# Summing the last expert's part on the residual in PSUM, in a two-layer trunk on one core

## The chip, the cores and the metric

The kernel runs on one core of one Trainium2 chip, as one launch. Its time is the device time of that core in microseconds (us); of a kernel several runs are taken, and the median stands for it. All engines of the core work from their own instruction queues, in order: TensorE (PE, with its weight loads shown as PEld), VectorE (DVE), ScalarE (ACT), GpSimd (POOL) and SyncE (SP), which issues most of the transfers.

## The reference, cut to what matters

Two layers. Layer 1 ends with a top-2-of-8 expert mixer, a layer norm over a scaled residual, and a gated embedding:

```python
def moe_swiglu(h, w_router, w1, w3, w2):
    ...
    for e in range(N_EXPERTS):
        out = out + gates[:, e:e + 1] * swiglu(t, w1[e], w3[e], w2[e])

# in reference(), layer i
f = moe_swiglu(x, router_w[j], exp_w1[j], exp_w3[j], exp_w2[j])
x = layer_norm(DEEPNORM_ALPHA * x + f, ln2_g[i], ln2_b[i])
x = x + jax.nn.sigmoid(x @ ple_gate_w[i]) * (p[i] @ ple_w[i])
```

There are 256 tokens, 1024 channels, 3584 hidden channels in an expert. Everything is float32 at its ends.

## The kernel before

The tokens are worked in two halves of 128 (`h` = 0, 1), each a tile of 128 partitions by 1024 channels, and the channels in two parts of 512 (`c` = 0, 1), since one PSUM bank holds 512 float32 a partition. A product of two float32 values is made from parts: weights and activations are split into a high part of the type fp32r and a rest (`H`, `L`), and a product is two or three passes over these (L343, L345 or L343, L347, L348). Weights that are not split (`direct`) go as plain float32 (L340). Weights come in 1 MB transfers into slots of one pool (`w`), ScalarE copies the high part (L143), VectorE makes the rest (L158); `W.prepare` says at which place of the program this is queued.

The experts run in blocks of 512 hidden channels. Tokens are gathered for an expert by a product with a 0/1 selection, and its result is scattered back by a product with the transposed selection `selTs`. `evacuate` splits the sum of an expert's down products into `y.h` (tile `cat`) and `y.l` (tile `yc`). `scatter` makes, for each half and part, two products into a PSUM bank `ps_sc` (L808, L809) and has VectorE add it to the residual `yacc` in SBUF (L811). `yacc` starts as the scaled residual, so after the last scatter it holds what the last norm works on.

The end of layer 1, in `moe`, stands in this order, which is the order of each engine's queue (nothing reorders it):

1. scatter of the last expert for half 0, `norm_begin` on `yacc[0]`: statistics (L383), mean and variance (L385, L387), the power on GpSimd (L389)
2. three of the four embedding products `ps_ple` (`emit(3)`), and 20 products that only keep TensorE busy (`warm`, L308)
3. `norm_apply` part by part (L412 with the mean and the gain, L413 with the inverse deviation and the offset), after each part the transposes (`tr`, L331) and their split into `xH`, `xL` (L316, L317) with an unsplit copy (L319)
4. scatter of the last expert for half 1, the fourth embedding product (copied out by ScalarE at L440), the statistics of half 1, `norm_apply` of half 1 (both parts)
5. `embed_gate`: four gate products `ps_gate`, the first with split weights (half 0, part 0), then half 0 part 1 with direct weights; the transposes of half 1 lie inside it; then half 1. `combine` ends each: sigmoid (L1150), multiply, add (L1151, L1152), and the transfer to the output.

PSUM has eight banks here: four for `mmt` tiles, used in turn, and four named `acc0` to `acc3`. A call of `acc` without a number takes the next of the four; a call with a number takes that one. A bank that is taken anew waits until its former content has been read. Up to the last `embed_gate` there are 38 calls without a number (14 in each mixer, 4 in the dense layer, 4 in the first `embed_gate`, 2 in `moe`), so its first product takes `acc2`, and the next ones `acc3`, `acc0`, `acc1`, `acc2`.

Of the kernel before, what the change touches and what calls it, by code (L numbers as in the profile page):

```python
# [13 lines left out]
ALU = mybir.AluOpType  # L14
# [179 lines left out]
def trunk(ctx: ExitStack, tc: tile.TileContext, a: dict, out: bass.AP):  # L194
    nc = tc.nc
# [9 lines left out]
    def acc(name, k=None):  # L205

        if k is None:
            k = at[0] % 4
            at[0] += 1
        return pacc.tile([P, 512], F32, tag=f"acc{k}", name=name)  # L210

    def mmt(name):
        return pmm.tile([P, 512], F32, tag="mm", name=name)

    def tl(tag, shape, dt=F32):
        return ap.tile([P] + shape, dt, tag=tag, name=tag)
# [73 lines left out]
    ident = con[:, C_ID:C_ID + P]  # L290
# [19 lines left out]
    def table(func):  # L310

        nc.scalar.activation(dummy, neghalf, func)

    def split_into(dst, src):

        nc.scalar.copy(dst.h, src)  # L316
        nc.vector.tensor_sub(dst.l, src, dst.h.bitcast(F32))  # L317
        if dst.f is not None:
            nc.scalar.copy(dst.f, src)  # L319

    def new_xT(f=None):
        return [Split(tl(f"xH{h}", [KD, P], F32R), tl(f"xL{h}", [KD, P], F32R), None if f is None else f[:, h])
                for h in range(2)]
# [10 lines left out]
    def to_xT(dst, src, c):  # L334

        split_into(dst[:, 4 * c:4 * c + 4, :], transposes(src[:, c * 512:(c + 1) * 512], 4))
# [43 lines left out]
    def norm_scalars(srcs):  # L380
        st = sm.tile([P, 2, 6], F32, tag="st", name="st")
        for i, s_ in enumerate(srcs):
            nc.vector.bn_stats(st[:, i], s_())  # L383
        mv = sm.tile([P, 2], F32, tag="mv", name="mv")
        nc.vector.bn_aggr(mv, st[:, :len(srcs)].rearrange("p a b -> p (a b)"))  # L385
        ve = sm.tile([P, 1], F32, tag="ve", name="ve")
        nc.vector.tensor_scalar_add(ve, mv[:, 1:2], EPS)  # L387
        rs = sm.tile([P, 1], F32, tag="rs", name="rs")
        nc.gpsimd.tensor_tensor(rs, ve, neghalf, op=ALU.pow)  # L389
        return mv[:, 0:1], rs  # L390
# [7 lines left out]
    def norm_begin(x, psums, between=None):  # L398

        cs = [x[:, c * 512:(c + 1) * 512] for c in range(2)]  # L400
        def add(c):
            if c and between:
                between()
            if psums is not None:
                nc.vector.scalar_tensor_tensor(cs[c], cs[c], ALPHA, psums[c], op0=ALU.mult, op1=ALU.add)
            return cs[c]
        return norm_scalars([lambda: add(0), lambda: add(1)])

    def norm_apply(gb, x, scalars, c):
        cs = slice(c * 512, (c + 1) * 512)  # L410
        mu, rs = scalars
        nc.vector.scalar_tensor_tensor(x[:, cs], x[:, cs], mu, gb[0][:, cs], op0=ALU.subtract, op1=ALU.mult)  # L412
        nc.vector.scalar_tensor_tensor(x[:, cs], x[:, cs], rs, gb[1][:, cs], op0=ALU.mult, op1=ALU.add)  # L413

    def norm(gb, x, psums):
        sc = norm_begin(x, psums)
        for c in range(2):
            norm_apply(gb, x, sc, c)
# [379 lines left out]
    def evacuate(accs):  # L798
        y = Split(tl("cat", [2, 512], F32R), tl("yc", [2, 512], F32R))
        for c in range(2):  # L800
            split_into(y[:, c, :], accs[c])
        return y

    def scatter(selT, y, yacc, k, halves=(0, 1)):
        for h in halves:
            for c in range(2):
                ps = acc("ps_sc", k + h) if c else mmt("ps_sc")
                nc.tensor.matmul(ps, selT[:, h], y.h[:, c], start=True, stop=False)  # L808
                nc.tensor.matmul(ps, selT[:, h], y.l[:, c], start=False, stop=True)  # L809
                yo = yacc[h][:, c * 512:(c + 1) * 512]  # L810
                nc.vector.tensor_add(yo, yo, ps)  # L811
# [27 lines left out]
    def moe(l, xr, gb1, mix, project):  # L839
        xT = new_xT()  # L840
        wrs = tl("s0", [KD, 2, NE], F32R)
        split_into(Split(wrs[:, :, 0], wrs[:, :, 1]), wr)
        project(0)
        norm(gb1, xr[0], mix[0])
        project(1, lambda k: k == 1 and to_xT(xT[0], xr[0], 0))
        sc = norm_begin(xr[1], mix[1], lambda: to_xT(xT[0], xr[0], 1))
        for c in range(2):
            norm_apply(gb1, xr[1], sc, c)
        table(AF.Sigmoid)

        p1 = [acc("p1") for _ in range(2)]
        lg = tl("lg", [2, NE])

        pr = [mmt("ps_r") for _ in range(2)]

        def router(h, ks):

            for k in ks:
                nc.tensor.matmul(pr[h][:, :2 * NE], xT[h].h[:, k, :], wrs[:, k].rearrange("p a e -> p (a e)"),
                                 start=k == 0, stop=False)  # L860
                nc.tensor.matmul(pr[h][:, :NE], xT[h].l[:, k, :], wrs[:, k, 0], start=False, stop=k == KD - 1)

        ids = W.names["w1e0_0"]
        proj(ids, p1[0], xT[0])
        to_xT(xT[1], xr[1], 0)
        router(0, range(KD))
        to_xT(xT[1], xr[1], 1)
        W.prepare("w3e0_0", 2)
        routed = []

        def routing(k):
            if k < 2:
                router(1, range(4 * k, 4 * k + 4))
            if k == 1:
                for h in range(2):
                    nc.vector.tensor_copy(lg[:, h], pr[h][:, NE:2 * NE])
                    nc.vector.tensor_add(lg[:, h], lg[:, h], pr[h][:, :NE])
                routed.extend(route(lg))
            if k == KP:
                gate, msk = routed  # L880
                routed.extend(positions(msk, gate, xr))

        proj(ids, p1[1], xT[1], free=True, also=routing)
        gate, msk, posm, cnt = routed
        sel, cc = select(0, posm, gate, 0, 0)
        W.prepare("w3e0_0")
        W.hl = HL_SECOND
        ss = [silu(p1[h], 512, h) for h in range(2)]
        W.cap = W.names[f"gate1{l}"][-1] + 1
        selT, gsl = turn_select(sel, 0), gate_select(sel, cc, 0)  # L890
        xg = gather(sel, xr, 0)
        ps = mmt("ps_s")
        for h in range(2):
            nc.tensor.matmul(ps, sel[:, h], ss[h], start=h == 0, stop=h == 1)
        s_ = tl("g1", [512])
        nc.scalar.copy(s_, ps)
        (ranks, gates), beyond, ci = order(cnt, posm, gate)
        p3 = mmt("p3")
        both("w3e0_0", [p3], [xg])
        g = glu(s_, p3, 512, 0, gsl)  # L900
        W.hl = HL_MOE
        yacc2 = W.temp([2, D])
        yacc = [yacc2[:, h] for h in range(2)]
        late = {}

        def end(c):

            if c == PLE_AT:
                late["ple"] = embedding(l)
            if c == GAINS_AT:  # L910
                late["gains"] = gains(l, "ln2", D)
            if c == FE:
                W.prepare(f"ple{l}", None)
                late["ple"][2]()

        last = experts(ranks, gates, xr, yacc, (selT, gsl, xg), lambda: hidden(g, 512, 0),
                       lambda: over(ci, beyond, gate, xr, yacc), end)
        gb, (ple, emit, _) = late["gains"], late["ple"]
        xT2 = new_xT(W.temp([2, KD, P]))
        table(AF.Sigmoid)  # L920
        last(0)
        sc = [norm_begin(yacc[0], None)]
        W.prepare(f"gate0{l}", 1)
        emit(EM[0])
        keep_warm(20)
        norm_apply(gb, yacc[0], sc[0], 0)
        to_xT(xT2[0], yacc[0], 0)
        norm_apply(gb, yacc[0], sc[0], 1)
        W.prepare(f"gate0{l}", 2)
        to_xT(xT2[0], yacc[0], 1)  # L930
        emit(EM[1])
        last(1)
        W.prepare(f"gate0{l}", 3)
        emit(4 - EM[0] - EM[1])
        sc.append(norm_begin(yacc[1], None))
        W.prepare(f"gate0{l}", 4)
        for c in range(2):
            norm_apply(gb, yacc[1], sc[1], c)
        W.prepare(f"gate1{l}")
        return xT2, yacc, lambda c: to_xT(xT2[1], yacc[1], c), ple  # L940

# [97 lines left out]
    def experts(ranks, gates, xr, yacc, nxt, first, more, end):  # L1039
# [4 lines left out]
        selTs, state = [nxt[0], None], {0: nxt[1:]}  # L1044
# [4 lines left out]
        for i, (e, c) in enumerate(BLOCKS):  # L1049
# [39 lines left out]
            pe, pc, paccs, pgT = prev  # L1089
# [46 lines left out]
        pe, pc, paccs, pgT = prev  # L1136
        down(W.names[f"w2e{pe}_{pc}"], paccs, pgT, False, True, True)
        end(FE)
        y = evacuate(paccs)
        return lambda h: scatter(selTs[1], y, yacc, 2 * (pe % 2), (h,))  # L1140

    def embed_gate(l, xT, late, xr, ple, last):

# [175 lines left out]
```

## Time and profile before

| | |
|---|---|
| median of 3 runs | 1354.1 us (1352.34 to 1355.91) |
| the profiled execution | 1351.87 us |
| its span, from the first to the last instruction | 1350.0 us |
| TensorE busy | 1314.0 us, 97% of the span |
| VectorE busy | 1169.0 us, 87% |
| ScalarE busy | 920.9 us, 68% |
| mean granted TensorE clock | 0.996 |

Busy time of an engine is the union of its instructions' times. The share of the whole span says what kind of kernel it is; what the end of the program costs is read from the timeline of its last 50 us, engine by engine, and from what ended the idle time ahead of an instruction. The granted clock is 1.00 where TensorE runs at its full level of 2.4 GHz and 0.5 at its lower one of 1.2 GHz.

### The profile page before, as it was taken

Reading aid. Unit: us, or ns where it says so; the run is one execution under the profiler, and the core shown is the slowest. Engines: PE = TensorE matmul, PEld = TensorE weight load, DVE = VectorE, ACT = ScalarE, POOL = GpSimd, SP = SyncE. Lnnn points to the kernel's source line nnn. Section 1 sums busy time; section 2 is a strip of 40 time slices with the busy share of each in tenths; the row PEclk is TensorE's granted clock in tenths of the full one; section 3 lists DMA queues with packets and bytes.
Section 4 is the critical chain, followed back from the end, with each engine's and each line's share of the span. In section 5 each row is a group of like instructions: output and inputs, shape, how many; then the busy total and the mean of one; then the engine's idle time right before and its main releaser. Section 6 shows DMA issues by size and latency. Waiting matters only on the chain. (4 is left out here: it accounts for less than half of the span.)

```text
span 1350.0 us, 17064 instructions
## 1 busy us (share of the span) xinstructions
PE 1314.0 (97%) x6310; PEld 1078.3 (80%) x6310; DVE 1169.0 (87%) x1098; ACT 920.9 (68%) x864; POOL 18.4 (1%) x31
## 2 busy tenths in 40 slices
PE   9999999999999999999999999999999999999788
PEld 7878888888868888878888878888887888888656
DVE  6987544567888989999999999999999999999874
ACT  6435444436425778878888887888887888898652
POOL 0000000010000000000000000000000000000000
PEclk9999999999999999999999999999999999999899
DMA  9546555446654889999999999999999999999850
GB/s 367 221 137 242 213 187 187 164 138 252 222 187 154 322 333 421 421 401 377 420 414 383 421 420 372 411 420 405 393 420 402 379 420 406 399 373 419 358 217 31
DMA packets 62171, 433.09 MB, mean 321 GB/s; under 512 B 6960, under 2 KB 7472, under 8 KB 11008
## 3 DMA queue, kind: packets, MB, share of 16 engines
q1 hardware_dynamic: 60336, 425.60, 79.9%
q0 software_dynamic: 1168, 4.23, 1.0%
q10 hardware_dynamic: 576, 2.10, 0.4%
q8 instruction: 51, 0.84, 0.2%
q14 instruction: 40, 0.33, 0.1%
HBM read 430.85 MB, written 1.05 MB: 320 GB/s over the span
## 5 line engine op out<-in xcount | busy, mean ns | idle before, releaser
L158 DVE TENSOR_TENSOR w<-w 128x2048 fp32r<-128x2048 f32 (+1 forms) x456 | 886.5, 1992 | 57.7 <-ACT w L143 51.0
L143 ACT CAST w<-w 128x2048 fp32r<-128x2048 f32 (+1 forms) x456 | 746.8, 1677 | 125.6 <-PE p L347 41.5
L343 PE MATMUL p<-w,xH 128*128 128x512 f32 (+1 forms) x1096 | 432.5, 395 | 7.5 <-DVEq L1034 6.0
L347 PE MATMUL p<-w,xH 128*128 128x512 f32 (+1 forms) x648 | 249.1, 384 | 0.4 <-DVE w L158 0.4
L348 PE MATMUL p<-w,xL 128*128 128x512 f32 (+1 forms) x648 | 249.5, 385 | 0.0
L343 PEld LDWEIGHTS p<-w,xH 128*128 128x128 f32 x1096 | 206.8, 189 | 49.4 <-issue 6.6
L343 PE MATMUL y<-w,gH 128*128 128x512 f32 x448 | 175.4, 392 | 2.5 <-DVE gH L378 2.5
L345 PE MATMUL p<-w,xH 128*128 128x512 f32 x448 | 175.9, 393 | 0.0
L348 PEld LDWEIGHTS p<-w,xL 128*128 128x128 f32 x648 | 121.8, 188 | 24.7
L347 PEld LDWEIGHTS p<-w,xH 128*128 128x128 f32 x648 | 122.0, 188 | 24.2 <-DVE w L158 0.8
L343 PEld LDWEIGHTS y<-w,gH 128*128 128x128 f32 x448 | 84.1, 188 | 20.9 <-DVE gH L378 3.6
L345 PEld LDWEIGHTS p<-w,xH 128*128 128x128 f32 x448 | 85.1, 190 | 17.0
L348 PE MATMUL y<-w,gL 128*128 128x512 f32 x224 | 87.4, 390 | 0.5 <-DVE gL L317 0.5
L347 PE MATMUL y<-w,gH 128*128 128x512 f32 x224 | 87.3, 390 | 0.0
L345 PE MATMUL y<-w,gH 128*128 128x512 f32 x224 | 87.3, 390 | 0.0
L483 DVE SCALAR_TENSOR_TENSOR yc<-w,vec,yc 128x256 f32<-128x256 f32 x176 | 70.4, 479 | 0.0
L646 ACT ACTIVATE s<-p 128x512 f32<-128x512 f32 (+1 forms) x69 | 41.1, 599 | 24.3 <-PE p L348 24.3
L316 ACT CAST gH<-tr 128x512 fp32r<-128x512 f32 x38 | 21.9, 588 | 47.9 <-PE tr L331 47.3
L317 DVE TENSOR_TENSOR gL<-tr,gH 128x512 fp32r<-128x512 f32 x38 | 25.7, 685 | 32.7 <-ACT gH L316 32.7
L348 PEld LDWEIGHTS y<-w,gL 128*128 128x128 f32 x224 | 42.1, 188 | 9.6 <-DVE gL L317 0.9
L347 PEld LDWEIGHTS y<-w,gH 128*128 128x128 f32 x224 | 42.1, 188 | 9.0
L345 PEld LDWEIGHTS y<-w,gH 128*128 128x128 f32 x224 | 42.1, 188 | 8.6
(227 smaller groups left out, 1391.7 us busy)
## 6 DMA issues: line engine op xcount, KB each, us to landing
w<-in_exp_w SPq DMA_DIRECT2D x336, 1024.0 KB, 8.8
w<-in_dense_w SPq DMA_DIRECT2D x33, 1024.0 KB, 5.1
w<-in_w_out SPq DMA_DIRECT2D x8, 1024.0 KB, 8.7
w<-in_ple_gate_w SPq DMA_DIRECT2D x8, 1024.0 KB, 5.9
w<-in_w_gv SPq DMA_DIRECT2D x6, 1024.0 KB, 6.9
w<-in_w_u SPq DMA_DIRECT2D x4, 1024.0 KB, 10.5
w<-in_w_gv SPq DMA_DIRECT2D x4, 512.0 KB, 6.8
w<-in_w_small SPq DMA_DIRECT2D x2, 1024.0 KB, 10.1
```

Source lines behind the costliest of these rows:

```text
L143: nc.scalar.copy(h, w)
L158: engine.tensor_tensor(l, w, h.bitcast(F32), op=ALU.subtract)
L316: nc.scalar.copy(dst.h, src)
L317: nc.vector.tensor_sub(dst.l, src, dst.h.bitcast(F32))
L343: nc.tensor.matmul(ps, x.h, wh, start=start, stop=False)
L345: nc.tensor.matmul(ps, x.h, wl, start=False, stop=stop)
L347: nc.tensor.matmul(ps, x.h, wl, start=False, stop=False)
L348: nc.tensor.matmul(ps, x.l, wh, start=False, stop=stop)
L483: nc.vector.scalar_tensor_tensor(yc[:, ct], src, weight(ct, t), yc[:, ct], op0=ALU.mult, op1=ALU.add)
L646: nc.scalar.activation(s_[:, :nf], p1[:, :nf], AF.Silu)
```

## The change

Only the last expert's scatter and the norm behind it are touched. Instead of a product into `ps_sc` and an addition on VectorE, a bank `ps_sum` first takes the residual itself, as a product of `yacc` with the identity in plain float32 (`residual`), and then the two selection products on top. The norm's statistics and the first step of `norm_apply` read that bank. The four VectorE additions are gone. For half 0 the identity products are queued ahead of `evacuate`; for half 1 they stand directly ahead of its selection products. The banks are named by number: `acc0` and `acc1` for half 0, `acc2` and `acc3` for half 1. Lines from 409 on move: L412 and L413 become L413 and L414, L440 becomes L441, L1150 becomes L1169.

```diff
-    def norm_apply(gb, x, scalars, c):
+    def norm_apply(gb, x, scalars, c, src=None):
         cs = slice(c * 512, (c + 1) * 512)
+        src = x[:, cs] if src is None else src
         mu, rs = scalars
-        nc.vector.scalar_tensor_tensor(x[:, cs], x[:, cs], mu, gb[0][:, cs], op0=ALU.subtract, op1=ALU.mult)
+        nc.vector.scalar_tensor_tensor(x[:, cs], src, mu, gb[0][:, cs], op0=ALU.subtract, op1=ALU.mult)
...
-        last(0)
-        sc = [norm_begin(yacc[0], None)]
+        sums = [last(0)]
+        sc = [norm_scalars([lambda c=c: sums[0][c] for c in range(2)])]
...
-        norm_apply(gb, yacc[0], sc[0], 0)
+        norm_apply(gb, yacc[0], sc[0], 0, sums[0][0])
...
-        last(1)
+        sums.append(last(1))
...
-        sc.append(norm_begin(yacc[1], None))
+        sc.append(norm_scalars([lambda c=c: sums[1][c] for c in range(2)]))
...
+        sums = {}
+        def residual(h):
+            sums[h] = [acc("ps_sum", 2 * h + c) for c in range(2)]
+            for c in range(2):
+                nc.tensor.matmul(sums[h][c], ident, yacc[h][:, c * 512:(c + 1) * 512], start=True, stop=False)
+        def last(h):
+            if h:
+                residual(h)
+            for c in range(2):
+                nc.tensor.matmul(sums[h][c], selTs[1][:, h], y.h[:, c], start=False, stop=False)
+                nc.tensor.matmul(sums[h][c], selTs[1][:, h], y.l[:, c], start=False, stop=True)
+            return sums[h]
+        residual(0)
         y = evacuate(paccs)
-        return lambda h: scatter(selTs[1], y, yacc, 2 * (pe % 2), (h,))
+        return last
```

TensorE's queue behind the transposes of half 0, part 1, in the difference of the two programs (- before, + now; `ps_sc` and `ps_sum` are the PSUM banks, `w` is the residual `yacc`, `con` holds the identity, `cat` and `yc` the split result of the expert; in brackets the engines waited for, _49 being part of a semaphore's name):

```order
 L331 MATMUL tr<-con,w 128x128 x3
-L808 MATMUL ps_sc<-cat,m_9306 128x512 [waits PE_49]
-L809 MATMUL ps_sc<-yc,m_9306 128x512
-L808 MATMUL ps_sc<-cat,m_9306 128x512
-L809 MATMUL ps_sc<-yc,m_9306 128x512
+L1146 MATMUL ps_sum<-w,con 128x512 x2
+L1153 MATMUL ps_sum<-cat,m_9306 128x512
+L1154 MATMUL ps_sum<-yc,m_9306 128x512
+L1153 MATMUL ps_sum<-cat,m_9306 128x512
+L1154 MATMUL ps_sum<-yc,m_9306 128x512
 L343 MATMUL ps_ple<-w 128x512 [waits PE_49]
```

Two identity products are new between the transposes and the selection products; for half 0 the same two stand between the last down product and the selection products.

TensorE's queue at the first gate product of half 0 (`ps_gate_13550`; the weights `w_13423` and `w_13502` are its first and second quarter), before:

```order
L343 MATMUL ps_gate_13550<-w_13423,xH0_13401 128x512 [waits Activation_49]
L347 MATMUL ps_gate_13550<-w_13423,xH0_13401 128x512
L348 MATMUL ps_gate_13550<-w_13423,xL0_13402 128x512
L343 MATMUL ps_gate_13550<-w_13423,xH0_13401 128x512
L347 MATMUL ps_gate_13550<-w_13423,xH0_13401 128x512
L348 MATMUL ps_gate_13550<-w_13423,xL0_13402 128x512
L343 MATMUL ps_gate_13550<-w_13502,xH0_13401 128x512 [waits Activation_49]
L347 MATMUL ps_gate_13550<-w_13502,xH0_13401 128x512 [waits DVE_49]
```

and now:

```order
L343 MATMUL ps_gate_13550<-w_13423,xH0_13405 128x512 [waits DVE_49,Activation_49]
L347 MATMUL ps_gate_13550<-w_13423,xH0_13405 128x512
L348 MATMUL ps_gate_13550<-w_13423,xL0_13406 128x512
L343 MATMUL ps_gate_13550<-w_13423,xH0_13405 128x512
L347 MATMUL ps_gate_13550<-w_13423,xH0_13405 128x512
L348 MATMUL ps_gate_13550<-w_13423,xL0_13406 128x512
L343 MATMUL ps_gate_13550<-w_13502,xH0_13405 128x512 [waits Activation_49]
L347 MATMUL ps_gate_13550<-w_13502,xH0_13405 128x512
```

The first product has a wait for VectorE that it did not have, and the waits for VectorE at the rests of the three later quarters of the weights are gone.

VectorE's queue for half 1, before (`ps_sc_13513` and `ps_sc_13517` are the scattered parts, `w_3562` the residual, `mv` and `rs` the norm's scalars, `w_13523` and `w_13543` the third and fourth quarter of the gate's weights):

```order
L811 TENSOR_TENSOR w_3562<-w_3562,ps_sc_13513 128x512 [waits PE_49]
L811 TENSOR_TENSOR w_3562<-w_3562,ps_sc_13517 128x512 [waits PE_49]
L158 TENSOR_TENSOR w_13523<-w_13311,w_13523 128x1024 [waits DMAHW7_49,Activation_49]
L383 BN_STATS st_13534<-w_3562 128x6 [waits DVE_49] x2
L385 BN_AGGR mv_13537<-st_13534 128x2 [waits DVE_49]
L387 TENSOR_SCALAR ve_13539<-mv_13537 128x1 [waits DVE_49]
L158 TENSOR_TENSOR w_13543<-w_13311,w_13543 128x1024 [waits Activation_49]
L412 SCALAR_TENSOR_TENSOR w_3562<-w_3562,mv_13537,w_13268 128x512
```

and now:

```order
L158 TENSOR_TENSOR w_13523<-w_13311,w_13523 128x1024 [waits DMAHW7_49,Activation_49]
L383 BN_STATS st_13534<-ps_sum_13513 128x6 [waits PE_49]
L383 BN_STATS st_13534<-ps_sum_13514 128x6 [waits PE_49]
L385 BN_AGGR mv_13537<-st_13534 128x2 [waits DVE_49]
L387 TENSOR_SCALAR ve_13539<-mv_13537 128x1 [waits DVE_49]
L158 TENSOR_TENSOR w_13543<-w_13311,w_13543 128x1024 [waits Activation_49]
L413 SCALAR_TENSOR_TENSOR w_3562<-ps_sum_13513,mv_13537,w_13268 128x512
```

The additions are gone from the front of it; the last reader of `ps_sum_13513` stands behind the rest of the fourth quarter (L158 of `w_13543`). ScalarE's queue has the same rows in the same order: the copy of the fourth embedding product, then the high part of `w_13543`.

## Rows read from the trace of the kernel before

**Rows 1.** The page's first section: busy time and share of the span.

```profile
PE 1314.0 (97%) x6310; PEld 1078.3 (80%) x6310; DVE 1169.0 (87%) x1098; ACT 920.9 (68%) x864; POOL 18.4 (1%) x31
```

**Rows 2.** Windows: length, busy us and count by engine, granted clock, DMA, GB/s.

```profile
1255.60:1259.00 3.40, 3.40 (x15) 2.82 (x16) 3.40 (x2) 3.26 (x3) 0.00 (x0) 1.00 1.01 422
1268.00:1272.00 4.00, 4.00 (x10) 3.04 (x10) 2.91 (x2) 0.04 (x1) 0.00 (x0) 0.50 0.90 317
1316.90:1320.10 3.20, 3.20 (x9) 2.51 (x8) 2.74 (x5) 1.72 (x3) 0.00 (x0) 0.50 0.00 0
1320.40:1345.90 25.50, 25.50 (x104) 18.52 (x102) 12.14 (x20) 5.86 (x10) 1.40 (x1) 1.00 0.09 36
```

**Rows 3.** Timeline of PE, half 0: start, length, line, operation, count, idle before.

```profile
1301.59 0.39 PE L345 MATMUL y<-w,gH 128*128 128x512 f32 x1
...
1303.53 0.50 PE L809 MATMUL ps_sc<-yc,m 128*128 128x512 f32 x1
1303.87 0.40 PE L343 MATMUL ps_ple<-w 128*128 128x512 f32 x1
...
1307.97 4.49 PE L308 MATMUL warm<-con 128*128 128x512 bf16 x20
1312.30 0.60 PE L331 MATMUL tr<-con,w 128*128 128x128 f32 x4
```

**Rows 4.** Timeline of PE, half 1 and the first gate products.

```profile
1315.84 0.63 PE L331 MATMUL tr<-con,w 128*128 128x128 f32 x4 [2.94 <-DVE w L413]
1316.22 0.47 PE L808 MATMUL ps_sc<-cat,m 128*128 128x512 f32 x1
...
1317.63 0.63 PE L343 MATMUL ps_ple<-w 128*128 128x512 f32 x1
...
1319.77 0.57 PE L348 MATMUL ps_ple<-w 128*128 128x512 f32 x1
1320.17 0.40 PE L343 MATMUL ps_gate<-w,xH 128*128 128x512 f32 x1
...
1325.64 6.17 PE L340 MATMUL ps_gate<-w 128*128 128x512 f32 x14
1331.64 0.60 PE L331 MATMUL tr<-con,w 128*128 128x128 f32 x4
```

**Rows 5.** Timeline of DVE, half 1.

```profile
1317.73 1.27 DVE L811 TENSOR_TENSOR w<-w,ps_sc 128x512 f32<-128x512 f32 x2
1319.41 1.23 DVE L158 TENSOR_TENSOR w<-w 128x1024 fp32r<-128x1024 f32 x1 [0.40 <-ACT w L143]
1320.55 1.28 DVE L383 BATCH_NORM_STATS2 st<-w 128x6 f32<-128x512 f32 x2
...
1322.18 1.22 DVE L158 TENSOR_TENSOR w<-w 128x1024 fp32r<-128x1024 f32 x1
1323.31 0.75 DVE L412 SCALAR_TENSOR_TENSOR w<-w,mv 128x512 f32<-128x512 f32 x1
```

**Rows 6.** Timeline of ACT: third quarter's high part, embedding copy, fourth quarter's.

```profile
1318.33 1.05 ACT L143 CAST w<-w 128x1024 fp32r<-128x1024 f32 x1
1320.43 0.59 ACT L440 COPY w<-ps_ple 128x512 f32<-128x512 f32 x1 [1.05 <-PE ps_ple L348]
1320.91 1.05 ACT L143 CAST w<-w 128x1024 fp32r<-128x1024 f32 x1
```

**Rows 7.** VectorE forms by line: durations in ns, min/median/max, PSUM (`ps_t`) or SBUF (`w`).

```profile
L383 DVE BATCH_NORM_STATS2 st<-ps_t x4: 691/692/693, 70.7 to 380.4; 128x6 f32<-128x512 f32 x4
L383 DVE BATCH_NORM_STATS2 st<-w x4: 674/681/689, 1304.7 to 1321.2; 128x6 f32<-128x512 f32 x4
...
L602 DVE SCALAR_TENSOR_TENSOR s<-ps_t,mv,w x4: 740/741/742, 71.7 to 381.4; 128x512 f32<-128x512 f32 x4
```

**Rows 8.** Timeline of PE: two earlier waits, with the idle time before them.

```profile
1255.58 0.50 PE L343 MATMUL y<-w,gH 128*128 128x512 f32 x1 [1.39 <-DVE gH L378]
...
1267.60 0.77 PE L343 MATMUL p<-w,xH 128*128 128x512 f32 x1 [6.00 <-DVEq L1034]
```

More of the change, by code (lines that the diff above doesn't have):

```diff
@@ L925, in moe @@
         keep_warm(20)
-        norm_apply(gb, yacc[0], sc[0], 0)
+        norm_apply(gb, yacc[0], sc[0], 0, sums[0][0])
         to_xT(xT2[0], yacc[0], 0)
-        norm_apply(gb, yacc[0], sc[0], 1)
+        norm_apply(gb, yacc[0], sc[0], 1, sums[0][1])
         W.prepare(f"gate0{l}", 2)
@@ L931, in moe @@
         emit(EM[1])
-        last(1)
+        sums.append(last(1))
         W.prepare(f"gate0{l}", 3)
         emit(4 - EM[0] - EM[1])
-        sc.append(norm_begin(yacc[1], None))
+        sc.append(norm_scalars([lambda c=c: sums[1][c] for c in range(2)]))
         W.prepare(f"gate0{l}", 4)
         for c in range(2):
-            norm_apply(gb, yacc[1], sc[1], c)
+            norm_apply(gb, yacc[1], sc[1], c, sums[1][c])
         W.prepare(f"gate1{l}")
```

## The prediction, made before the changed kernel ran

> **What bounds the kernel now.** I read the share of busy time first, only to see where to look: TensorE is busy for 97% of the span [rows 1], so the end of the program is TensorE's queue plus whatever makes it wait. The change touches only the last 50 us, so the rest of the reading is the timeline of that stretch. From the first gate product at 1320.17 on [rows 4], TensorE does not stop: in the window from 1320.40 to 1345.90 it is busy 25.50 of 25.50 us [rows 2]. After that come a sigmoid, two VectorE steps and the last transfer, which the change leaves alone. So the span, 1350.0 us, is the start of the first gate product plus a fixed 29.83 us, and every edit is to be priced by what it does to that start. In front of it stand, on TensorE, the down products, the scatter of half 0, three embedding products, the 20 keep-busy products, two groups of transposes, the scatter of half 1 and the fourth embedding product [rows 3, 4].
>
> VectorE, whose additions the change removes, is not what TensorE waits for in most of this. In half 0 its norm has the 4.49 us of keep-busy products as cover [rows 3]. In half 1 its two additions are followed by 0.40 us of waiting for ScalarE [rows 5], and before the change no TensorE instruction near by waits for the norm of half 1: the gate products of half 0 run beside it, and half 1's transposes come at 1331.64 [rows 4], 7 us after it. That is the first reason for doubt: what is removed, four additions of 0.64 us [rows 5], lies beside other work; what is added lies on TensorE.
>
> **The change part by part.**
>
> *The price of an identity product.* The trace has the same form already: plain float32, 128 by 128 on 128x512, in the direct gate products. Seven of them are 14 records in 1331.64 - 1325.64 = 6.00 us [rows 4], so 0.857 us each. A pass over split values takes (1325.64 - 1320.17)/24 = 0.228 us [rows 4], so a pair of identity products, 1.714 us, is worth some seven and a half such passes.
>
> *Half 0.* The last down product starts at 1301.59 and frees its place 0.23 us later, at 1301.82 [rows 3]. Before, TensorE then waited for the split of the expert's sum, and the embedding products began at 1303.87. Now the identity products fill 1301.82 to 1303.53. By then the split is done: the last scatter pass, which waits for its last piece, started at 1303.53 [rows 3]. Four passes of 0.228 follow, and the embedding products begin at 1304.44: **0.57 us later**. The wait for the split is the cover that hides the other 1.14 us. VectorE starts its statistics some 0.4 us earlier for lack of the additions, but the transposes stand behind the keep-busy products anyway, so that is worth nothing. Everything to the second group of transposes moves by 0.57 us, from 1315.84 to 1316.41.
>
> *Reading PSUM instead of SBUF.* Statistics take 692 ns from PSUM and 681 from SBUF, and the first step of a norm 741 ns from PSUM [rows 7] against 0.75 us from SBUF [rows 5]: nothing. The Trainium skill ("VectorE: DVE Perf Modes", section "Why PSUM operands drop a tier") says that an operand in PSUM keeps VectorE out of its faster two-port mode, which would speak against this change; if that doubled the two statistics of half 1 it would add 1.4 us, and by the rows just named it adds 0.02, since they show no faster mode from SBUF.
>
> *Half 1, on TensorE.* The scatter's passes started 0.38 us after the transposes [rows 4]; now the identity products do, at 1316.79. In this execution TensorE's granted clock fell to half behind the 2.94 us of idling in front of these transposes: 0.50 in the window from 1316.90 to 1320.10 [rows 2], with passes of (1319.77 - 1317.63)/5 = 0.43 us until 1320.17 [rows 4]. With the same fall at the same place, four identity records take 0.857 us each and end at 1320.22; the ten passes behind them run at 0.228 us; the last embedding pass starts at 1322.27 and lands 0.39 us later, at 1322.66, against 1319.77 + 0.57 = 1320.34 [rows 4]: **2.3 us later**.
>
> *Half 1, the new wait.* This is the term that decides. The bank of the first gate product is `acc2`: 38 unnumbered calls stand ahead of it, and 38 mod 4 is 2. `acc2` is now also `ps_sum` of half 1, part 0, and its last reader is the first step of `norm_apply` for half 1. The order of TensorE agrees: that product has gained a wait for VectorE, and the later waits for the rests of the gate's weights have vanished, as they would if it waited for something behind all of them; in VectorE's order this reader stands behind the last of them. So TensorE stops at the first gate product until that step is over, and behind it stand all gate products and the transposes of half 1. What ends last in front of that step is a chain through three engines that was harmless before: the fourth embedding product lands, ScalarE copies it 0.09 us later, starts the high part of the fourth weight quarter 0.48 us after that and takes 1.05 us [rows 6], VectorE makes the rest (it followed ScalarE by 0.03 us for the third quarter: 1319.41 [rows 5] against 1318.33 + 1.05 = 1319.38 [rows 6]), 1.13 us from its start to that of the norm's step, which takes 0.75 [rows 5], and 0.09 us for the wake-up, as for the copy. That is 3.62 us: 1322.66 + 3.62 = 1326.28, where the product started at 1320.17 before: **6.1 us later**, the 2.3 included.
>
> If neither version has a fall of the clock here, the result is the same: before, ten passes behind 1316.22 would end at 1318.50; now the embedding product lands at 1320.95 and the chain ends at 1324.57, while the norm's own path (third quarter's rest 0.57 us later at 1319.98, statistics 1.14 us behind it, the norm's step 2.76 us behind those and 0.75 long [rows 5]) ends at 1324.72: 6.2 us later. Only if the fall hits the old kernel and spares the new one is it 1324.72 - 1320.17 = 4.5 us.
>
> The Trainium skill ("PSUM — Partial Sum Buffer", section "Summary: rules for kernel authors") advises to evacuate promptly; a bank kept until a norm has its scalars is the opposite. No row of the kernel before shows such a hold.
>
> *The clock behind the new wait.* TensorE has nothing to do from 1322.50 (the last embedding pass and its place) to 1326.28, 3.8 us. An idle time of 1.39 us, ending at 1255.58 [rows 8], had no fall behind it: 1.00 in the window from 1255.60 [rows 2]. 2.94 us had one [rows 2, 4]. 6.00 us, ending at 1267.60 [rows 8], had one: 0.50 in the window from 1268.00 [rows 2]. 3.8 lies between the two that had one, so I expect a fall. Its price: the stretch behind 2.94 us ran at half from 1316.78 to 1320.17, 3.4 us in which half the work is lost, **1.7 us**. Bounds: nothing, and from the stretch behind 6.00 us, at least 4.0 us at 0.50 [rows 2], some 2.0 to 2.4.
>
> *Sum.* The profiled execution took 1351.87 us: 1351.87 + 6.1 + 1.7 = 1359.7. It lies 2.2 us under the median of the runs, 1354.1, so on the scale of the median the forecast is 1354.1 + 7.8 = **1361.9 us**.
>
> **The rivals.**
>
> *The wait without the fall.* If 3.8 us of idling is split so that the clock stays up, only the wait remains: 1354.1 + 6.1 = 1360.2, or 1358.6 with the 4.5 above. For it: 1.39 us cost nothing, and the three runs before differ by 3.6 us, which falls at other places from run to run could explain. Against it: 2.94 us was enough.
>
> *The wait ends early (not slower).* The order names the engine waited for, not the instruction. If the first gate product waited for half 0's norm only, which is over long before, TensorE would run on at 1322.50 instead of 1320.17: 2.3 us, 1356.4, less than the 0.3% (4.1 us) that a measurement of this kernel can tell from no change. It decides at one point, the bank of the first gate product: any but `acc2` and `acc3`, and this case holds. Against it stand the count of calls and the vanished waits.
>
> *A longer fall.* As behind the 6.00 us: 6.1 + 2.4 gives 1362.6.
>
> *A gain.* It would need identity products of the price of one pass and no wait; even then 0.46 us stay on the path of half 1, with nothing of VectorE's saving in front of it. I see no mechanism, and leave 3 in 100.
>
> **How the numbers follow.** Forecast 0.60, the wait without the fall 0.22, the early end 0.09, the longer fall 0.06, a gain 0.03. The predicted time is the forecast's, 1361.9. The range must hold the forecast and the two cases beside it: from 1358.6 less 0.8 to 1362.6 plus 1.4, for the scatter of medians of runs that lie within 1.8 us of their own: 1357.8 to 1364.0. The early end and a gain, 0.12, stay outside. Slower by over 0.3% (above 1358.2): 0.60 + 0.06 + 0.19 of the 0.22 = 0.85. Within 0.3%: 0.09 + 0.03 = 0.12. Faster: 0.03.
>
> **What the profile after would show.** The identity products as four records of 0.43 us behind the last down product, and embedding products 0.5 to 0.6 us later. The first gate product with an idle time of 3 to 4 us in front of it, released by VectorE's first norm step on `ps_sum`; in front of that step, without idling, the rest of the fourth quarter; in front of that, ScalarE's high part and the copy of `ps_ple`. Granted clock near 0.5 for some 3 us among the first gate products. A span of some 1357.8 us. I am wrong on the main term if the first gate product follows the embedding products without idling, on the second if the clock stays at 1.00 behind it, and on the first if the identity products are not 0.86 us each.

## The result and the profile after

| | before | after |
|---|---|---|
| median | 1353.98 us of 4 runs (1352.34 to 1355.91) | 1361.75 us of 4 runs (1360.44 to 1362.69) |
| the profiled execution | 1351.87 us | 1362.63 us |
| its span | 1350.0 us | 1360.5 us |

The ratio of after to before is 1.0053, with a 95% interval of 1.0042 to 1.0065: slower by 7.8 us. The prediction was 1361.9.

The two profiled executions differ by 10.76 us, more than the medians do. The last down product starts at 1301.59 before [rows 3] and at 1304.10 after. That is 2.51 us in front of any instruction that the change touches, and the same kind of difference shows between all the executions below: that start lies anywhere from 1301.59 to 1304.96 with the same program ahead of it. Most of it is a fall of TensorE's clock some 880 us ahead of the change, which only some of the executions had. The window from 415 to 432, before and after (length; busy us and count by engine PE, PEld, DVE, ACT, POOL; granted clock, DMA share, GB/s):

```profile
415.00:432.00 17.00, 16.14 (x97) 13.56 (x97) 13.29 (x50) 10.03 (x15) 0.00 (x0) 1.00 0.66 247
415.00:432.00 17.00, 16.14 (x92) 13.92 (x92) 11.89 (x42) 8.40 (x14) 0.00 (x0) 0.90 0.67 247
```

A clock of 0.90 over 17 us is 1.7 us of work lost, of the 2.51. In the ten profiled executions of this document the window is at 1.00 (before, e1_banks, f1_idle, f4_added: the last down product starts at 1301.59 to 1302.67), at 0.90 (after, e2_half0, f3_before_short: 1303.12 to 1304.10) or at 0.80 (e3_filled, e4_quarter, f2_short: 1304.58 to 1304.96). So from here on times are counted from the start of the last down product (the **tail**): 48.41 us before, 56.40 after, 7.99 more. Of the 10.76 the last 0.26 lies outside the spans.

TensorE's timeline after, from the last down product on (start, length, line, operation, count, idle before and who ended it; `...` marks rows left out); it answers to [rows 3] and [rows 4]:

```profile
1304.10 0.39 PE L345 MATMUL y<-w,gH 128*128 128x512 f32 x1
1304.33 1.88 PE L1146 MATMUL ps_sum<-w,con 128*128 128x512 f32 x4
1305.64 0.79 PE L1153 MATMUL ps_sum<-cat,m 128*128 128x512 f32 x1
...
1306.97 0.39 PE L343 MATMUL ps_ple<-w 128*128 128x512 f32 x1
...
1311.08 4.49 PE L308 MATMUL warm<-con 128*128 128x512 bf16 x20
1315.40 0.60 PE L331 MATMUL tr<-con,w 128*128 128x128 f32 x4
1318.94 0.63 PE L331 MATMUL tr<-con,w 128*128 128x128 f32 x4 [2.94 <-DVE w L414]
1319.40 3.26 PE L1146 MATMUL ps_sum<-w,con 128*128 128x512 f32 x4
...
1324.87 0.39 PE L348 MATMUL ps_ple<-w 128*128 128x512 f32 x1
1328.94 0.47 PE L343 MATMUL ps_gate<-w,xH 128*128 128x512 f32 x1 [3.69 <-DVE w L413]
...
1336.11 6.17 PE L340 MATMUL ps_gate<-w 128*128 128x512 f32 x14
```

Read it in four steps. The identity products stand right behind the last down product, and the embedding products begin 2.87 us into the tail, where they began 1303.87 - 1301.59 = 2.28 before [rows 3]: 0.59 more. Both groups of transposes are 0.59 later too (11.30 and 14.84 against 10.71 and 14.25). The first gate product starts at 24.84 against 18.58 [rows 4], 6.26 more, with 3.69 us of idling in front. And from it to the direct products are 1336.11 - 1328.94 = 7.17 us against 5.47 [rows 4], 1.70 more, although the same 24 passes lie there.

The wait itself, from the table of waits after, behind 1304 (who waited, for whom: total us, times, longest):

```profile
PE ps_gate L343 <- DVE w L413: 3.7, 1, 3.7
```

The end of VectorE's work for half 1, after; it answers to [rows 5]:

```profile
1322.51 1.23 DVE L158 TENSOR_TENSOR w<-w 128x1024 fp32r<-128x1024 f32 x1 [1.59 <-ACT w L143]
1323.65 1.29 DVE L383 BATCH_NORM_STATS2 st<-ps_sum 128x6 f32<-128x512 f32 x2
...
1325.22 0.15 DVE L387 TENSOR_SCALAR ve<-mv 128x1 f32<-128x1 f32 x1
1326.91 1.22 DVE L158 TENSOR_TENSOR w<-w 128x1024 fp32r<-128x1024 f32 x1 [1.54 <-ACT w L143]
1328.05 0.74 DVE L413 SCALAR_TENSOR_TENSOR w<-ps_sum,mv,w 128x512 f32<-128x512 f32 x1
```

What had to come first, from the chain of work that ended last, after (start, us, what; without the pieces of waiting):

```profile
1325.35 0.58 ACT w L441
1325.93 0.95 ACT w L143
...
1326.91 1.22 DVE w L158
1328.13 0.67 DVE w L413
...
1328.94 0.47 PE ps_gate L343
```

L441 is the copy of the fourth embedding product, L143 a high part, L158 a rest. That is the chain the prediction named, link by link: the copy of the fourth embedding product, the high part of the fourth weight quarter, its rest, the norm's step that reads `ps_sum`, and only then the gate. The step's scalars were not late: VectorE had `ve` at 1325.37, and waited 1.54 us for ScalarE, not for GpSimd.

The clock, from the windows of after (length; busy us and count by engine; granted clock, DMA share, GB/s); it answers to [rows 2]:

```profile
1330.11:1333.31 3.20, 3.20 (x10) 2.46 (x9) 0.95 (x2) 0.00 (x0) 0.00 (x0) 0.50 0.00 0
1336.11:1342.11 6.00, 6.00 (x15) 2.60 (x14) 1.39 (x2) 0.60 (x1) 0.00 (x0) 1.00 0.11 44
```

TensorE stays at half for 3.2 us, beginning 1.2 us behind the first gate product.

Reading PSUM costs VectorE next to nothing, as the groups by form of after show (count; busy us, mean ns of one); they answer to [rows 7], with 681 ns for the statistics from SBUF there and 0.75 us for the norm's step in [rows 5]:

```profile
L413 DVE SCALAR_TENSOR_TENSOR w<-ps_sum,mv,w 128x512 f32<-128x512 f32 x4 | 3.0, 744 | 0.0
...
L383 DVE BATCH_NORM_STATS2 st<-ps_sum 128x6 f32<-128x512 f32 x4 | 2.6, 688 | 0.7 <-PE ps_sum L1154 0.7
```

### The profile page after: what moved, and what is told of

Its sections match the earlier page's. It is cut to its first block, busy times and chain, and to the rows that moved or that the text cites. A ratio compares the mean times of both kernels' runs of the same rounds, so it can differ in the third digit from the quotient of the medians.

```text
span 1360.5 us, 17077 instructions
## 1 busy us (share of the span) xinstructions
PE 1320.8 (97%) x6318; PEld 1082.6 (80%) x6318; DVE 1166.5 (86%) x1094; ACT 920.9 (68%) x864; POOL 17.5 (1%) x31
## 5 line engine op out<-in xcount | busy, mean ns | idle before, releaser
L158 DVE TENSOR_TENSOR w<-w 128x2048 fp32r<-128x2048 f32 (+1 forms) x456 | 886.2, 1990 | 61.0 <-ACT w L143 54.6
L143 ACT CAST w<-w 128x2048 fp32r<-128x2048 f32 (+1 forms) x456 | 746.7, 1677 | 126.1 <-PE p L347 41.4
L647 ACT ACTIVATE s<-p 128x512 f32<-128x512 f32 (+1 forms) x69 | 41.1, 599 | 24.3 <-PE p L348 24.3
```

The costliest lines, as they stand in the source:

```text
L143: nc.scalar.copy(h, w)
L158: engine.tensor_tensor(l, w, h.bitcast(F32), op=ALU.subtract)
L647: nc.scalar.activation(s_[:, :nf], p1[:, :nf], AF.Silu)
```

## The experiments

**Theory:** the 7.8 us are three things in a row: identity products on TensorE (2.3 us), a wait of the first gate product for the bank that the norm still reads (3.8), and the fall of the clock behind that wait (1.7). **Rivals:** that the bank is not what holds the gate, so that naming another changes nothing; that reading PSUM or the identity products cost more than their share; that the clock would have fallen anyway. The first four runs take one term away each; the last four ask what is to be had in this tail. All eight compute the full result. The times in the tail, in us from the start of the last down product:

| kernel | embedding products | transposes, 1st / 2nd group | first gate product | direct products | end of span | median, and before beside it |
|---|---|---|---|---|---|---|
| before | 2.28 | 10.71 / 14.25 | 18.58 | 24.05 | 48.41 | 1353.98 |
| after | 2.87 | 11.30 / 14.84 | 24.84 | 32.01 | 56.40 | 1361.75 (1353.98) |
| e1_banks | 2.87 | 11.30 / 14.84 | 21.00 | 26.45 | 50.79 | 1355.35 (1353.75) |
| e2_half0 | 2.87 | 11.30 / 14.84 | 19.21 | 24.67 | 49.08 | 1355.02 (1353.75) |
| e3_filled | 2.87 | 11.31 / 14.84 | 24.76 | 30.34 | 54.74 | 1360.20 (1353.75) |
| e4_quarter | 2.87 | 11.30 / 14.84 | 23.41 | 28.97 | 53.38 | 1358.73 (1353.75) |
| f1_idle | 2.87 | 11.31 / 14.84 | 16.69 | 22.32 | 46.66 | 1352.64 (1354.85) |
| f2_short | 2.87 | 7.85 / 11.39 | 13.24 | 18.87 | 43.22 | 1349.79 (1354.85) |
| f3_before_short | 2.27 | 7.59 / 11.16 | 15.49 | 20.97 | 45.33 | 1350.62 (1354.85) |
| f4_added | 2.27 | 7.59 / 11.15 | 14.28 | 20.06 | 44.43 | 1349.15 (1354.85) |

The median less the tail is between 1304.6 and 1306.6 for all ten, so the tail of one profiled execution accounts for the medians to about a microsecond. Each kernel has one trace. Smaller differences, and those between kernels whose intervals overlap (after, e3_filled and e4_quarter), are read from the tails alone.

### Another bank for the gate

After, with two turns of the bank counter skipped at the end of `moe`, so that the first gate product takes `acc0`, which half 0's norm has long left:

```diff
             norm_apply(gb, yacc[1], sc[1], c, sums[1][c])
+        at[0] += 2
         W.prepare(f"gate1{l}")
```

> One line on top of the changed kernel: the turn of the four accumulator banks is moved on by two ahead of the gate products, so that the first gate product of half 0 takes acc0 and not acc2. The identity products, the reads of PSUM by the norm and the missing additions stay. Theory (a bank held until the norm of half 1 has read it, then idling, then a fall of the clock): the wait of 3.7 us in front of the first gate product and the half-clock stretch among the gate products are both gone, and only the identity products' 0.6 + 1.7 us stay: some 2.3 us above the kernel before, 1356.3 us. Rival (the norm's reads of PSUM or the identity products themselves cost the 7.8 us): no change against the changed kernel, 1361.75 us.

Measured: 1355.35 us (1354.61 to 1358.3, 11 runs), ratio 1.0017 (1.0008 to 1.0026). TensorE's timeline of this kernel at the place of the wait:

```profile
1323.09 0.39 PE L348 MATMUL ps_ple<-w 128*128 128x512 f32 x1
1323.31 0.39 PE L343 MATMUL ps_gate<-w,xH 128*128 128x512 f32 x1
...
1328.76 6.17 PE L340 MATMUL ps_gate<-w 128*128 128x512 f32 x14
```

The gate follows the embedding product without idling, and the direct products come 5.45 us later, at full clock. One bank number is worth 56.40 - 50.79 = 5.61 us of tail (7.77 - 1.60 = 6.2 by the medians against their own before): the wait, 24.84 - 21.00 = 3.84, and the fall, 7.17 - 5.45 = 1.72. What is left, 2.38 us over before, is the identity products.

### Half 0 alone

After, with half 1 scattered into `ps_sc` and added by VectorE as before:

```diff
-        sc.append(norm_scalars([lambda c=c: sums[1][c] for c in range(2)]))
+        sc.append(norm_begin(yacc[1], None))
...
-            norm_apply(gb, yacc[1], sc[1], c, sums[1][c])
+            norm_apply(gb, yacc[1], sc[1], c)
...
             if h:
-                residual(h)
+                return scatter(selTs[1], y, yacc, 2 * (pe % 2), (h,))
```

> Half of the change alone: half 0 is summed in PSUM on identity products as in the changed kernel, half 1 is scattered and added on VectorE as before. Theory: the identity products of half 0 are hidden by the wait for the split but for 0.6 us, and nothing is held: 1354.6 us, within 0.3% of the kernel before. Rival (identity products cost their full 1.7 us a half, since the wait for the split is paid anyway): 1355.7 us. If most of the loss lay in half 0: near 1360 us.

Measured: 1355.02 us (1352.81 to 1356.22, 11 runs), ratio 1.0006 (0.9997 to 1.0015); by the runs alone it can't be told from no change. The trace can: embedding products, transposes and first gate product are 0.59, 0.59 and 0.63 us later than before, and the tail is 0.67 longer. Against e1_banks, half 1's identity products make 21.00 - 19.21 = 1.79 us.

### The wait filled with products

After, with 14 of the keep-busy products between the fourth embedding product and the first gate product:

```diff
         emit(4 - EM[0] - EM[1])
+        keep_warm(14)
```

> The changed kernel with 14 keep-busy products (some 3.0 us) queued on TensorE between the fourth embedding product and the first gate product, inside the 3.7 us in which it waits for VectorE. Theory (the clock falls because of that idling): the wait stays as long as it was, the half-clock stretch behind it is gone, 1.7 us less: 1360.0 us, and the granted clock is 1.00 among the first gate products. Rival (the clock falls there for another reason, or the fall costs nothing since something else ends last): 1361.75 us as before.

Measured: 1360.2 us (1359.44 to 1361.81, 5 runs), ratio 1.0049 (1.0035 to 1.0062). TensorE's timeline:

```profile
1325.97 3.20 PE L308 MATMUL warm<-con 128*128 128x512 bf16 x14
1329.72 0.50 PE L343 MATMUL ps_gate<-w,xH 128*128 128x512 f32 x1 [0.56 <-DVE w L413]
...
1335.30 6.17 PE L340 MATMUL ps_gate<-w 128*128 128x512 f32 x14
```

and the window from its first gate product to the direct ones (length; busy by engine; granted clock, DMA share, GB/s):

```profile
1329.72:1335.30 5.58, 5.58 (x25) 4.62 (x26) 2.17 (x3) 0.00 (x0) 0.00 (x0) 1.00 0.00 0
```

The gate starts where it did in after (24.76 against 24.84): the products do not shorten the wait. They keep the clock at 1.00, and the tail is 1.66 us shorter. So in these traces the clock's term comes from the idling, and it is this size.

### The fourth quarter ahead of the copy

After, with ScalarE's copy of the fourth embedding product queued behind the high part of the fourth weight quarter. TensorE's and VectorE's queues are those of after:

```diff
-        emit(4 - EM[0] - EM[1])
         sc.append(norm_scalars([lambda c=c: sums[1][c] for c in range(2)]))
         W.prepare(f"gate0{l}", 4)
+        emit(4 - EM[0] - EM[1])
```

> The changed kernel with two ScalarE instructions exchanged: the high part of the gate's fourth weight quarter stands ahead of the copy of the fourth embedding product; TensorE's and VectorE's queues are word for word the same. Theory (what ends last in front of the norm's first step is the chain embedding product, copy, fourth quarter's high part, its rest): the rest starts right behind the variance instead of 1.5 us later, the first gate product starts 1.6 us earlier, after 2.1 us of idling: 1360.1 us if the clock still falls behind that, 1358.4 us if not. Rival (the norm's own path ends last and the fourth quarter is beside it): no change, 1361.75 us.

Measured: 1358.73 us (1357.09 to 1360.45, 5 runs), ratio 1.0039 (1.0025 to 1.0054). TensorE's timeline:

```profile
1328.23 0.47 PE L343 MATMUL ps_gate<-w,xH 128*128 128x512 f32 x1 [2.22 <-DVE w L413]
```

and VectorE's in front of it:

```profile
1324.57 1.29 DVE L383 BATCH_NORM_STATS2 st<-ps_sum 128x6 f32<-128x512 f32 x2
...
1326.21 1.22 DVE L158 TENSOR_TENSOR w<-w 128x1024 fp32r<-128x1024 f32 x1
1327.34 0.74 DVE L413 SCALAR_TENSOR_TENSOR w<-ps_sum,mv,w 128x512 f32<-128x512 f32 x1
```

Two ScalarE instructions exchanged, and the rest of the quarter no longer idles 1.54 us: the wait is 1.43 us shorter (23.41 against 24.84). So the path to the gate did run through ScalarE's copy, as predicted; what is late next is VectorE's own work on half 1. The clock did not fall behind the 2.22 us left (5.56 us to the direct products), which the expectation had left open.

### Half 1's sum in the earlier idle time

e1_banks, with half 1's identity and selection products moved ahead of the second group of transposes, where TensorE idles for 2.94 us, and the two last weight quarters ahead of half 1's statistics:

```diff
         to_xT(xT2[0], yacc[0], 0)
+        sums.append(last(1))
         norm_apply(gb, yacc[0], sc[0], 1, sums[0][1])
         W.prepare(f"gate0{l}", 2)
         to_xT(xT2[0], yacc[0], 1)
         emit(EM[1])
-        sums.append(last(1))
         W.prepare(f"gate0{l}", 3)
+        W.prepare(f"gate0{l}", 4)
         emit(4 - EM[0] - EM[1])
         sc.append(norm_scalars([lambda c=c: sums[1][c] for c in range(2)]))
-        W.prepare(f"gate0{l}", 4)
```

> The changed kernel with the banks moved on by two, half 1's identity and selection products queued ahead of the second group of transposes (TensorE idles 2.9 us there, waiting for the norm of half 0), and the gate's third and fourth weight quarter prepared ahead of half 1's statistics. Theory (the identity products of half 1 cost only where they stand, and the fall of the clock follows the idling): the 2.6 us of products fit into the idling, 0.5 us of it remains, the clock does not fall, the fourth embedding product follows the transposes at once and the direct gate products start 22.1 us after the last down product (24.05 before): 2.0 us below the kernel before, 1351.8 us. Rival (identity products delay the end wherever they stand): at or above 1355.4 us, as with the banks alone.

Measured: 1352.64 us (1350.66 to 1355.14, 11 runs), ratio 0.9988 (0.9979 to 0.9997). TensorE's timeline:

```profile
1316.78 0.63 PE L331 MATMUL tr<-con,w 128*128 128x128 f32 x4 [0.30 <-DVE w L414]
```

Of the 2.94 us of idling 0.30 is left, and no fall follows it. Against e1_banks the gate is 4.31 us earlier: 2.64 of filled idle time, which leaves 1.67 for the fall that is gone. The direct products came 0.2 us later than expected, since the 24 passes took 5.63 us and not 5.45, at a clock of 1.00. The table of waits for this stretch, 1318.6 to 1325, has one that e1_banks doesn't show, for the rest of a weight quarter:

```profile
PEld ps_gate L347 <- DVE w L158: 0.3, 1, 0.3
```

The gate is now early enough to meet VectorE's work on its weights. The median is 0.8 us above the 1351.8 that was expected.

### Fewer keep-busy products

In f1_idle, and in the kernel before, 4 of them in place of 20:

```diff
-        keep_warm(20)
+        keep_warm(4)
```

> As the one before, and 4 keep-busy products instead of 20. Theory (the norm of half 0 is done 6.98 us after the last down product and the first transposes only wait for the keep-busy products): they start 3.45 us earlier, and so does everything behind them: 1348.3 us. Rival (the keep-busy products cover a norm that takes as long, or without them the clock falls): 1351.8 us or more.

> The kernel before with 4 keep-busy products instead of 20 and nothing else. Theory (the norm of half 0, additions included, is done 7.45 us after the last down product, the transposes start at 10.71 us): the first transposes start at 7.6 us, 3.1 us earlier: 1350.7 us, with the fall of the clock behind the 2.9 us of idling as it was. Rival (the cover is needed): no gain, 1353.75 us, or a second fall, 1355 us. It prices what hid the VectorE additions of half 0: with less cover the additions become part of the path.

Measured: f2_short 1349.79 us (1348.56 to 1350.83, 5 runs), ratio 0.9962 (0.9948 to 0.9976); f3_before_short 1350.62 us (1349.37 to 1351.45, 6 runs), ratio 0.9967 (0.9954 to 0.9979). In f2_short's trace the transposes start 3.46 us earlier than in f1_idle's and the tail is 3.44 shorter, as expected; the median is 1.5 us above the expected 1348.3. In the trace of the kernel before, VectorE's second norm step of half 0 (L413, 0.75 us from 1308.29) ends 7.45 us into the tail, and the transposes that it feeds start at 10.71, behind the 20 products. With four products TensorE still waits for the norm for only 0.18 us; the timeline of f3_before_short:

```profile
1309.95 1.04 PE L308 MATMUL warm<-con 128*128 128x512 bf16 x4
1311.16 0.63 PE L331 MATMUL tr<-con,w 128*128 128x128 f32 x4 [0.18 <-DVE w L413]
1314.73 0.63 PE L331 MATMUL tr<-con,w 128*128 128x128 f32 x4 [2.94 <-ACT w L143]
```

The transposes come 3.12 us earlier in the tail (7.59 against 10.71), and that is 3.08 us at its end. The idle time of 2.94 us and the fall behind it are as before.

### The same place with additions

The kernel before, with 4 keep-busy products, half 1's selection products in the earlier idle time, and VectorE's two additions behind the rests of the third and fourth quarter. That is f2_short without identity products and without sums in PSUM:

```diff
-        keep_warm(20)
+        keep_warm(4)
...
         to_xT(xT2[0], yacc[0], 0)
+        parts = []
+        last(1, parts)
...
-        last(1)
         W.prepare(f"gate0{l}", 3)
+        W.prepare(f"gate0{l}", 4)
         emit(4 - EM[0] - EM[1])
+        for c in range(2):
+            yo = yacc[1][:, c * 512:(c + 1) * 512]
+            nc.vector.tensor_add(yo, yo, parts[c])
         sc.append(norm_begin(yacc[1], None))
-        W.prepare(f"gate0{l}", 4)
```

> The kernel before, without identity products: half 1's selection products ahead of the second transposes, its two VectorE additions behind the gate's third and fourth quarter, 4 keep-busy products. It differs from the short identity version in how the residual is added alone. Theory: TensorE saves half 0's 0.6 us, VectorE pays its additions on the now shorter path of half 0, 0.4 us; the direct gate products start 18.4 us after the last down product against 18.6: 1348.1 us, the same as the identity form within 0.5 us. Rival (the missing additions are the worth of the change once the cover is gone): slower than the short identity version by the two additions, 1.3 us or more.

Measured: 1349.15 us (1347.82 to 1350.98, 5 runs), ratio 0.996 (0.9946 to 0.9973). By the traces f2_short's tail is 1.21 us shorter, by the medians f4_added is 0.64 faster, and the intervals of the two overlap: by the runs no difference between the forms can be told. Both beat the kernel before by some 0.4%. The direct products were expected 18.4 us into the tail and came at 20.06. The timeline of f4_added shows that its idle time is only partly filled:

```profile
1313.82 0.77 PE L331 MATMUL tr<-con,w 128*128 128x128 f32 x4 [2.01 <-DVE w L413]
```

The clock fell behind it, as the windows show:

```profile
1313.82:1317.10 3.28, 3.28 (x11) 2.69 (x12) 1.91 (x2) 1.72 (x3) 0.00 (x0) 0.55 0.02 5
```

In f2_short the same transposes and embedding products ran at full clock behind 0.30 us of idling:

```profile
1315.97:1317.82 1.85, 1.85 (x11) 1.59 (x11) 1.79 (x2) 0.59 (x1) 0.00 (x0) 1.00 0.04 9
```

From the second transposes to the gate that is 1.85 us against 14.28 - 11.15 = 3.13 in f4_added, 1.28 more, and this covers the 1.21 of the tails. VectorE's additions are not what f4_added loses by: its second transposes start earlier (11.15 against 11.39). So the identity products stand free of charge where TensorE idles, and in these two traces they also filled that idle time far enough that no fall followed. Whether keep-busy products beside the additions would do the same was not tried. Of the tail before, 48.41, f3_before_short takes off 3.08 us by fewer keep-busy products alone, f4_added 3.98 and f2_short 5.19.

## Why the prediction was right

- **Where to look.** That everything is priced by the start of the first gate product, with the clock behind it as a term of its own, held: from that start to the end of the span are 29.83 us before and 31.56 after, and the 1.73 between them is the clock's. From the direct products on, the tails are 24.3 to 24.4 us long in all ten kernels.
- **Half 0's identity products:** predicted 0.57, measured 0.59 in after and in e2_half0. The cover was the wait for the split of the expert's sum, and it took the rest of the pair's 1.7 us.
- **VectorE's additions and its PSUM reads:** predicted at nothing, and the forms took 688 and 744 ns. The rule in the Trainium skill ("VectorE: DVE Perf Modes", section "Why PSUM operands drop a tier") makes no difference to these two float32 forms here.
- **Half 1's identity products:** predicted 2.3 with half 0's, measured 21.00 - 18.58 = 2.42 in e1_banks, where TensorE doesn't wait for the bank.
- **The wait:** predicted 3.8 us of idling and a gate 6.1 us later in all; measured 3.69 and 6.26. e1_banks shows that it was the bank, e4_quarter that the path to it went through ScalarE's copy. Counting the calls up to the gate gave the bank, and the vanished waits of the later quarters gave the place in VectorE's queue. The Trainium skill ("PSUM — Partial Sum Buffer", section "Summary: rules for kernel authors") advises prompt evacuation; after's 3.69 us agree with it where the next taker of the bank comes early, and e1_banks shows that the same hold costs nothing when another bank is taken.
- **The clock:** predicted 1.7, measured 1.70 in after, 1.66 and 1.72 when it was taken away. It was the least certain term, and e4_quarter shows that 1.5 us less of idling would have made the rival without the fall true. The reason given for it, that 3.8 us lie between two lengths that had a fall, is weaker than its success: 2.01 us in f4_added had a fall and 2.22 us in e4_quarter had none, so length alone does not order these cases.
- **The scale:** adding the terms to the median and not to the profiled execution was right. The 2.51 us by which the two executions differ ahead of the change spoil a comparison of spans: the span that the prediction named as a sign, 1357.8, was 1360.5. That the medians meet the forecast within 0.2 us is in part luck, since the interval of the ratio allows anything from 5.7 to 8.8 us for the change. The prediction held it possible that falls of the clock at other places make the runs of one kernel differ; the window from 415 to 432 shows one such place.

The case that the gate doesn't wait was put at 1356.4 us, and e1_banks, which makes it true, took 1355.35; the wait without the fall was put at 1360.2, and e3_filled, which makes that one true, took 1360.2.

## What to carry to other kernels

When a result is left in PSUM for a late reader, find out by the order of bank calls who takes that bank next: here one bank number was worth 5.6 us, and the reader was late for reasons that had nothing to do with it. Work moved from an engine with slack (four additions of 0.64 us) to the engine that sets the end was a loss here except where it fell into idle time there, so look for that idle time first, and see how much of it each form of the work fills. A run of products put in to keep TensorE busy is to be sized by the wait that it covers, and to be measured again when that wait changes.

## What was not expected of the hardware

Length alone does not say whether an idle time of TensorE is followed by a fall of the clock. Behind 2.22 us in e4_quarter the granted clock stayed at 1.00, as this window from its first gate product to the direct ones shows, and behind 2.01 us in f4_added it fell (0.55 in the window above):

```profile
1328.23:1333.79 5.56, 5.56 (x24) 4.59 (x25) 2.13 (x3) 0.00 (x0) 0.00 (x0) 1.00 0.00 0
```

In e4_quarter TensorE had run without a gap from 1319.66 on, for 6.3 us, some 3.4 of them at half the clock (0.52 from 1320.1 to 1323.5); in f4_added 3.6 us lie between the start of the first transposes and that of the second, 2.01 of them idle, with another short gap in front. Whether that is the reason was not tried.

GpSimd's power on 128 values (L389) took 1.42 us for half 0 and 0.55 for half 1 in the same execution of after, by its own timeline, whose spans are rough on this engine:

```profile
1308.58 1.42 POOL L389 TENSOR_TENSOR rs<-ve,neghalf 128x1 f32<-128x1 f32 x1 [23.26 <-DVE ve L387]
1325.51 0.55 POOL L389 TENSOR_TENSOR rs<-ve,neghalf 128x1 f32<-128x1 f32 x1 [15.51 <-DVE ve L387]
```

Before, both took 1.4. Nothing waited for it in after, so it moved no time. The ten traces show what goes with the length. It took 1.39 to 1.43 us in all 14 cases where VectorE was at work on the rest of a weight quarter (L158, from SBUF) beside it, and ended 0.39 to 0.43 us after that instruction. It took 0.55 where VectorE was idle (after, e1_banks and e3_filled, half 1) or ran the norm's first step from PSUM (f1_idle, f2_short). Beside the same step from SBUF, 0.74 us long, it took 0.92 in f4_added, and there VectorE's next step waited 0.44 us for it:

```profile
1322.63 0.74 DVE L412 SCALAR_TENSOR_TENSOR w<-w,mv 128x512 f32<-128x512 f32 x1
1322.86 0.92 POOL L389 TENSOR_TENSOR rs<-ve,neghalf 128x1 f32<-128x1 f32 x1 [13.83 <-DVE ve L387]
1323.82 0.75 DVE L413 SCALAR_TENSOR_TENSOR w<-w,rs 128x512 f32<-128x512 f32 x1 [0.44 <-POOL rs L389]
```

So it looks as if GpSimd's small operation waits for a VectorE instruction that reads SBUF; no run was made for this.
